# Differential attention: the two maps mixed at raised priority, and the output products issued as three of 128 columns into one sum

## The chip, the cores and the metric

The kernel runs on one core of one Trainium2 chip. The metric is the device time of one execution in microseconds, as the median of several runs. Before the change it is 1921.71 us (three runs, 1919.52 to 1921.93). The engines of a core work side by side and wait for each other through semaphores: TensorE (PE in the profile, with its weight loads shown apart as PEld), VectorE (DVE), ScalarE (ACT), GpSimd (POOL) and SyncE (SP), which issues most of the transfers from memory.

## The reference, cut to what matters

Two decoder layers of width 1024 over 512 tokens. Each layer runs a feed-forward network, a token mixer, a cross-attention into 256 memory tokens, and a second feed-forward network, each followed by a layer norm. The mixer of layer 0 is the differential attention, and the change lies in it alone:

```python
q = rope(q, c5, s5); k = rope(k, c5, s5)          # 8 heads, two maps c = 0, 1 of 64 dims each
s = jnp.einsum('bqhcd,bkhcd->bhcqk', qblk, k).astype(jnp.float32) * scale
s = jnp.where(mask, s, jnp.finfo(jnp.float32).min)
p = jax.nn.softmax(s, axis=-1)
a = p[:, :, 0] - lam * p[:, :, 1]
o = jnp.einsum('bhqk,bkhe->bqhe', a.astype(v.dtype), v)
...
o = o * lax.rsqrt(jnp.mean(jnp.square(o), axis=-1, keepdims=True) + LN_EPS)
o = o * subln_g.astype(jnp.float32) * (1.0 - lam_init)
return o.reshape(B, S, H * 2 * dk).astype(x.dtype) @ w_o
```

## The kernel before, in words

All matrix products keep close to float32 precision by splitting each operand into a high part (rounded to the 4-byte format float32r) and a low part (the rest). A product of two split operands is three matmuls that add into one sum in PSUM: high x high, high x low, low x high (`mm3`, lines 210 to 212). ScalarE makes the high part and VectorE the low part (`split`, lines 125 and 126; `cols_rope`, lines 280 and 283, for the weights of queries and keys).

The differential attention runs two generators side by side (`weave`). The main one (`da_main`) makes values, queries and keys, head by head, and at the end the first half of the output projection. The side one (`da_side`) goes through 8 heads x 4 blocks of 128 queries and issues, each a few steps behind the one before:

- `da_scores`: two maps of scores into PSUM tiles `sc` (lines 1125 and 1126); VectorE adds the mask and finds the row maximum (line 1131), ScalarE takes the exponential with the row sums (line 1134).
- `da_mix`: VectorE computes a reciprocal `rc`, a factor `cf`, and the mixture of both maps, `p[1] * cf + p[0]` (lines 1143 to 1145).
- `da_turn`: TensorE transposes the mixed block `p` into `pt` (line 494); it is split into `a[0]` (high, ScalarE) and `a[1]` (low, VectorE).
- `da_out`: TensorE multiplies it by the values into `po`, for two query blocks per PSUM bank. ScalarE copies half of `po` to `o`, VectorE adds the other half, and ScalarE squares `o` with a row sum into `sq`; after the fourth block GpSimd computes the scale `f`.
- `da_scale`, `da_turn_out`: ScalarE scales `o`, TensorE transposes it, and it is split into `oT`, the operand of the output projection.

The values `v` lie in SBUF as [high | low], 2 x 128 columns side by side. So one matmul with 256 columns yields `a[0]` x high and `a[0]` x low in two separate halves of `po` (line 1166), and a second one with 128 columns adds `a[1]` x high to the first half (line 1167); the two halves are added by VectorE (line 1173). There are 80 such pairs: 8 heads x (1 + 2 + 3 + 4) blocks of keys.

The order of instructions on each engine is set when the kernel is built: a list scheduler takes, among the instructions that it holds to be ready, the one of highest priority, which is by default the order of the program. Code under `self.tc.high_priority()` goes ahead of that. Each engine then works through its own list strictly in that order. TensorE's list in this stage follows the two generators.

PSUM tiles `sc`, `pt` and `po` come from one set of three names with two banks each, taken in turn (`aux`); a bank is used again when everything that reads or writes its tile is done. The squares are written to the first half of `po` (line 1176), a place that is never read.

Of the kernel before, what the change touches and what calls it, by code (L numbers as in the profile page):

```python
# [12 lines left out]
AF = mybir.ActivationFunctionType  # L13
ALU = mybir.AluOpType
# [3 lines left out]
P = 128  # L18
# [91 lines left out]
class Trunk:  # L110
# [80 lines left out]
    def mm(self, name):  # L191
        return self.mmp.tile([P, S], F32, tag="mm", name=name)
# [946 lines left out]
    def da_mix(self, st, i):  # L1139

        nc = self.nc
        p, sm, rc, cf = st.pop(("m", i))
        nc.vector.reciprocal(rc, sm[:, 1:2])
        nc.vector.scalar_tensor_tensor(cf, sm[:, 0:1], self.nlam, rc, ALU.mult, ALU.mult)
        nc.vector.scalar_tensor_tensor(p[0], p[1], cf, p[0], ALU.mult, ALU.add)
        st["p", i] = p[0]

    def da_turn(self, st, i):
# [8 lines left out]
    def da_out(self, st, i):  # L1157
        nc = self.nc
        if i == 0:
            st["o"], st["sq"] = self.tmp("o", (P, NT, P)), self.small("sq", (P, NT))  # L1160
        if i % 2 == 0:
            st["po"] = self.aux("po").rearrange("p (i s e) -> p i s e", i=2, s=2)
        a, o, po, mm = st.pop(("a", i)), st["o"], st["po"], nc.tensor.matmul
        for j in range(i + 1):
            v = st["v"][j][:, st["h"] % 2]
            mm(po[:, i % 2], a[0][:, j], v, start=j == 0, stop=False)
            mm(po[:, i % 2, 0], a[1][:, j], v[:, 0], start=False, stop=j == i)
        if i % 2 == 0:
            return
        o2 = o[:, i - 1 : i + 1]  # L1170
        with self.tc.high_priority():
            nc.scalar.copy(o2, po[:, :, 1])
            nc.vector.tensor_tensor(o2, o2, po[:, :, 0], ALU.add)
        sq = st["sq"]
        for i in range(i - 1, i + 1):
            nc.scalar.activation(
                po[:, 0, 0], o[:, i], AF.Square, scale=float(P**-0.5), accum_out=sq[:, i : i + 1]
            )
        if i < NT - 1:
            return  # L1180

        f, G, s0 = self.small("f", (P, NT)), nc.gpsimd, st["sm"][:, :, 0]
        G.tensor_scalar(f, s0, EPS, None, ALU.mult)
        G.tensor_tensor(f, f, s0, ALU.mult)
        G.tensor_tensor(f, f, sq, ALU.add)
        G.tensor_tensor(f, f, self.mhalf, ALU.pow)
        st["f"] = f
# [446 lines left out]

    def mixer(self, layer, ln):
        if layer == 0:
            bufs = dict(low=4, rt=2, a=4, p=6, o=2, qk=8, _x=0, v=4, oT=11, mask=1)
            with self.other_pools(), self.phase_pool(("v", "v"), "rt", **bufs):
                self.diff_attention(layer, ln)
            self.close_side()  # L1640
        else:
            self.later = ExitStack()
            self.later.enter_context(self.stage_pools(4, dict(raw=2), ("wh", "wl", "mem", "p", "raw")))
            self.to_w(self.later)
            self.kvp = self.later.enter_context(self.pool("kv"))
            bufs = dict(p=4, pw=1, gb=2, _x=0, pooled=16, sq=1)
            with self.phase_pool(("gb", "gb"), "sq", **bufs):
                side = self.pool_mixer(layer, ln)
                with self.tc.high_priority():
                    self.load_memory()  # L1650
                w = self.a["xa_wkv"][layer]
                raws = [self.raw_cols(w, c) for c in (0, D)]
                self.pool_bias()
                next(side)
                self.kv, self.keys, self.kv_bufs = [], [], 10
                self.weave(self.early_kv(layer, ln, 2, raws), side, 850, 8500)
            self.close_side()
# [46 lines left out]
```

## Time and profile before

| | us |
|---|---|
| median of 3 runs | 1921.71 |
| the profiled execution, its own time | 1921.52 |
| its span, first to last instruction | 1919.7 |
| differential attention with scores and outputs running, about 372 to 560 | 188 |

The profile shows the busy time of each engine, groups of equal instructions with their mean duration, who waited for whom, and instructions in order of time. Three points on reading it. A matmul's drawn end is modelled and overlaps the next ones: products of 256 columns start 0.12 us apart while each is drawn 0.28 us long, so what a matmul costs is read from starts, not from durations. A wait is shown as idle time before the instruction that waited, with the one that released it. And in the trace a matmul can be read twice, as its weight load (PEld) and as the product itself.

### The profile page before, as it was taken

To read this page: it belongs to the slowest core of one execution; us is meant where nothing else is said; L and a number is where in the kernel's file an instruction comes from. 1 tells how busy PE (TensorE), PEld (TensorE's weight loads), DVE (VectorE), ACT (ScalarE), POOL (GpSimd) and SP (SyncE) were. 2 spreads that over 40 slices of the span, in tenths; PEclk is the share of its full clock that TensorE was granted. 3 is DMA by queue.
4 is the path that set the end of the run, shared out by engine and by line. 5 is a ranking of instruction groups with operands and counts; after the bars stand their busy time and mean duration, and the time that the engine had idled before them with its cause. 6 is when DMAs were issued, how large, how long until landed. Compare 5 with 4: busy or idle time off the path is not lost.

```text
span 1919.7 us, 32489 instructions
## 1 busy us (share of the span) xinstructions
PE 1895.9 (99%) x13072; PEld 1738.2 (91%) x13072; DVE 1563.6 (81%) x2264; ACT 1023.4 (53%) x1580; POOL 319.8 (17%) x278
## 2 busy tenths in 40 slices
PE   9999999999999999999999999999999999999998
PEld 8999998888878888999998999999899889999997
DVE  7888889888867558889888988898787568998886
ACT  6555454567755435645554655455455436555552
POOL 3112121111210002221220311212130012111210
PEclk9999999999999999999999999999999999999999
DMA  9978772322224327987785587878344437877861
GB/s 250 213 173 179 175 140 78 91 66 88 66 88 154 110 66 195 180 179 162 144 192 180 108 180 164 183 164 183 108 132 132 133 87 162 174 168 167 186 133 55
DMA packets 246743, 277.96 MB, mean 145 GB/s; under 512 B 8256, under 2 KB 212544, under 8 KB 246592
## 3 DMA queue, kind: packets, MB, share of 16 engines
q0 software_dynamic: 92928, 92.29, 31.4%
q1 hardware_dynamic: 153664, 183.59, 29.8%
q8 instruction: 103, 1.69, 0.4%
q14 instruction: 48, 0.39, 0.1%
HBM read 273.75 MB, written 2.10 MB: 144 GB/s over the span
## 4 chain that ended last, share of the span: by engine, by line
PE 78%; DVE 13%; ACT 4%; DMA 2%; issue 2%; POOL 1%; SPq 0%; DVEq 0%; ACTq 0%; POOLq 0%
PE x L210 7%; PE x L211 7%; PE x L212 7%; PE z L212 4%; PE z L210 4%; PE z L211 4%; PE ps L210 4%; PE ps L212 4%; PE ps L211 4%; PE px L210 2%; PE px L212 2%; PE px L211 2%; PE y L212 2%; PE xq L210 1%; PE xq L211 1%
## 5 line engine op out<-in xcount | busy, mean ns | idle before, releaser
L685 POOL DMA_DIRECT2D ra<-in_ffn_w_in_dram x132 | 170.7, 1313 | 982.8 <-DVE wl L692 808.9
L690 ACT CAST wh<-ra 128x1024 fp32r<-128x1024 f32 x176 | 185.1, 1054 | 207.5 <-PE x L211 66.5
L692 DVE TENSOR_TENSOR wl<-ra,wh 128x1024 fp32r<-128x1024 f32 x176 | 213.9, 1220 | 67.1 <-ACT wh L690 66.4
L210 PE MATMUL x<-xe,wh 128*128 128x256 f32 x704 | 195.0, 277 | 0.0
L211 PE MATMUL x<-xe,wh 128*128 128x256 f32 x704 | 194.8, 277 | 0.0
L690 ACT CAST wh<-rc 128x1024 fp32r<-128x1024 f32 x132 | 138.9, 1053 | 104.9 <-PE x L211 40.4
L212 PE MATMUL x<-xe,wl 128*128 128x256 f32 x704 | 194.8, 277 | 0.0
L125 ACT CAST wh<-b 128x1024 fp32r<-128x1024 f32 x112 | 117.8, 1052 | 128.9 <-PE x L211 65.1
L692 DVE TENSOR_TENSOR wl<-rc,wh 128x1024 fp32r<-128x1024 f32 x132 | 159.8, 1218 | 26.8 <-ACT wh L690 26.8
L126 DVE TENSOR_TENSOR wl<-b,wh 128x1024 fp32r<-128x1024 f32 x112 | 136.6, 1220 | 40.2 <-ACT wh L125 40.2
L210 PE MATMUL x<-xh,wh 128*128 128x256 f32 x536 | 148.7, 277 | 0.0
L211 PE MATMUL x<-xl,wh 128*128 128x256 f32 x536 | 148.4, 277 | 0.0
L212 PE MATMUL x<-xh,wl 128*128 128x256 f32 x536 | 148.4, 277 | 0.0
L211 PEld LDWEIGHTS x<-xe,wh 128*128 128x128 f32 x704 | 132.5, 188 | 1.4
L210 PEld LDWEIGHTS x<-xe,wh 128*128 128x128 f32 x704 | 132.2, 188 | 1.3
L212 PEld LDWEIGHTS x<-xe,wl 128*128 128x128 f32 x704 | 132.2, 188 | 0.0
L126 DVE TENSOR_TENSOR wl<-raw,wh 128x1024 fp32r<-128x1024 f32 x64 | 83.0, 1300 | 42.4 <-ACT wh L125 41.6
L211 PEld LDWEIGHTS x<-xl,wh 128*128 128x128 f32 x536 | 100.9, 188 | 0.7
L210 PEld LDWEIGHTS x<-xh,wh 128*128 128x128 f32 x536 | 100.6, 188 | 0.7
L212 PEld LDWEIGHTS x<-xh,wl 128*128 128x128 f32 x536 | 100.6, 188 | 0.0
L125 ACT CAST wh<-raw 128x1024 fp32r<-128x1024 f32 x64 | 66.5, 1049 | 59.3 <-PE xq L211 21.0
L210 PE MATMUL z<-xe,wh 128*128 128x256 f32 x352 | 97.5, 277 | 0.0
(450 smaller groups left out, 6329.1 us busy)
## 6 DMA issues: line engine op xcount, KB each, us to landing
ra<-in_ffn_w_in_dram POOLq DMA_DIRECT2D x132, 512.0 KB, 7.0
rc<-in_ffn_w_in_dram SPq DMA_DIRECT2D x88, 512.0 KB, 5.7
b<-in_ffn_w_out_dram SPq DMA_DIRECT2D x76, 512.0 KB, 4.7
ra<-in_ffn_w_in_dram SPq DMA_DIRECT2D x44, 512.0 KB, 4.7
rc<-in_ffn_w_in_dram POOLq DMA_DIRECT2D x44, 512.0 KB, 8.0
raw<-in_xa_wkv_dram SPq DMA_DIRECT2D x16, 1024.0 KB, 5.4
raw<-in_da_w_qkv_dram SPq DMA_DIRECT2D x16, 512.0 KB, 5.3
raw<-in_xa_wq_dram SPq DMA_DIRECT2D x8, 1024.0 KB, 5.1
```

The costliest lines, as they stand in the source:

```text
L125: self.nc.scalar.copy(hi, src),
L126: self.nc.vector.tensor_sub(lo, src, hi.bitcast(F32)),
L210: mm(out, w[0], x[0], start=start, stop=False, skip_group_check=again)
L211: mm(out, w[0], x[1], start=False, stop=False, skip_group_check=again)
L212: self.last_mm = mm(out, w[1], x[0], start=False, stop=stop, skip_group_check=again)
L685: nc.gpsimd.dma_start(t, source(*block), accum_op=ALU.add)
L690: hi = nc.scalar.copy(v[0], raw)
L692: lo = nc.vector.tensor_sub(v[1], raw, v[0].bitcast(F32))
```

## The change

Three edits, all in the differential attention of layer 0.

1. `da_mix` issues its three VectorE instructions with raised priority.
2. `da_out` accumulates one 128-column result in PSUM with three matmuls of 128 columns per key block (`a[0]` x high, `a[0]` x low, `a[1]` x high) where there were one of 256 and one of 128 columns. `po` takes 2 x 128 columns of the bank instead of 2 x 2 x 128. VectorE's addition (line 1173) is gone; ScalarE's copy reads the finished sum.
3. The squares go to an SBUF tile `squares` of 128 x 128 with one buffer, not to `po`.

```diff
@@ da_mix
-        nc.vector.reciprocal(rc, sm[:, 1:2])
-        nc.vector.scalar_tensor_tensor(cf, sm[:, 0:1], self.nlam, rc, ALU.mult, ALU.mult)
-        nc.vector.scalar_tensor_tensor(p[0], p[1], cf, p[0], ALU.mult, ALU.add)
+        with self.tc.high_priority():
+            nc.vector.reciprocal(rc, sm[:, 1:2])
+            nc.vector.scalar_tensor_tensor(cf, sm[:, 0:1], self.nlam, rc, ALU.mult, ALU.mult)
+            nc.vector.scalar_tensor_tensor(p[0], p[1], cf, p[0], ALU.mult, ALU.add)
@@ da_out
-            st["po"] = self.aux("po").rearrange("p (i s e) -> p i s e", i=2, s=2)
+            st["po"] = self.aux("po")[:, : 2 * P].rearrange("p (i e) -> p i e", i=2)
...
-            mm(po[:, i % 2], a[0][:, j], v, start=j == 0, stop=False)
-            mm(po[:, i % 2, 0], a[1][:, j], v[:, 0], start=False, stop=j == i)
+            mm(po[:, i % 2], a[0][:, j], v[:, 0], start=j == 0, stop=False)
+            mm(po[:, i % 2], a[0][:, j], v[:, 1], start=False, stop=False)
+            mm(po[:, i % 2], a[1][:, j], v[:, 0], start=False, stop=j == i)
...
-            nc.scalar.copy(o2, po[:, :, 1])
-            nc.vector.tensor_tensor(o2, o2, po[:, :, 0], ALU.add)
-        sq = st["sq"]
+            nc.scalar.copy(o2, po)
+        sq, squares = st["sq"], self.tmp("squares", (P, P))
...
-                po[:, 0, 0], o[:, i], AF.Square, scale=float(P**-0.5), accum_out=sq[:, i : i + 1]
+                squares, o[:, i], AF.Square, scale=float(P**-0.5), accum_out=sq[:, i : i + 1]
@@ mixer
-            bufs = dict(low=4, rt=2, a=4, p=6, o=2, qk=8, _x=0, v=4, oT=11, mask=1)
+            bufs = dict(low=4, rt=2, a=4, p=6, o=2, qk=8, _x=0, v=4, oT=11, mask=1, squares=1)
```

The rest of this section shows where instructions stand now. In the changed kernel the lines of `da_mix` are 1144 to 1146 (one more than before), the three products are 1167 to 1169, and the copy and the squares are 1174 and 1177.

TensorE, head 0, the products of the third query block (three key blocks), among the query projection of a later head. Before:

```order
L212 MATMUL q<-xh,wl 128x512
L1166 MATMUL po<-v,a 128x256
L1167 MATMUL po<-v,a 128x128
L1166 MATMUL po<-v,a 128x256
L1167 MATMUL po<-v,a 128x128
L1166 MATMUL po<-v,a 128x256
L1167 MATMUL po<-v,a 128x128
L210 MATMUL q<-xh,wh 128x512
```

With the change:

```order
L212 MATMUL q<-xh,wl 128x512
L1167 MATMUL po<-v,a 128x128
L1168 MATMUL po<-v,a 128x128
L1169 MATMUL po<-v,a 128x128
L1167 MATMUL po<-v,a 128x128
L1168 MATMUL po<-v,a 128x128
L1169 MATMUL po<-v,a 128x128
L1167 MATMUL po<-v,a 128x128
L1168 MATMUL po<-v,a 128x128
L1169 MATMUL po<-v,a 128x128
L210 MATMUL q<-xh,wh 128x512
```

Six matmuls became nine, at the same place. Apart from this, TensorE's list is the same in both kernels up to the last head.

VectorE, an earlier head's last query block (its scores are the 128x512 ones): `rc`, `cf` and `p` are the mix, `a<-pt,a` the low part of a transposed block that TensorE waits for. Before:

```order
L1143 RECIPROCAL rc<-sd 128x1
L1144 SCALAR_TENSOR_TENSOR cf<-sd,nlam,rc 128x1
L1145 SCALAR_TENSOR_TENSOR p<-p,cf 128x512
L126 TENSOR_TENSOR a<-pt,a 128x256
L1131 ISA p,mx<-sc,mask 128x128
```

With the change:

```order
L1144 RECIPROCAL rc<-sd 128x1
L1145 SCALAR_TENSOR_TENSOR cf<-sd,nlam,rc 128x1
L126 TENSOR_TENSOR a<-pt,a 128x256
L1146 SCALAR_TENSOR_TENSOR p<-p,cf 128x512
L1131 ISA p,mx<-sc,mask 128x128
```

The low part of `a`, which has raised priority in both kernels, now stands ahead of the mixture.

VectorE, third query block of a later head (the block is 384 columns wide). `rt<-q` and `wl<-raw` belong to the main generator: the rotation of the next head's query, and low parts of weights. Before:

```order
L1143 RECIPROCAL rc<-sd 128x1
L1083 STREAM_SHUFFLE rt<-q 128x512
L1084 TENSOR_TENSOR rt<-q,ropeC 128x512
L126 TENSOR_TENSOR a<-pt,a 128x128
L1086 TENSOR_TENSOR rt<-rt 128x512
L1173 TENSOR_TENSOR o<-o,po 128x256
L1144 SCALAR_TENSOR_TENSOR cf<-sd,nlam,rc 128x1
L126 TENSOR_TENSOR wl<-raw,wh 128x1024
...
L1097 SCALAR_TENSOR_TENSOR qk<-rt,qk 64x512 x2
L1145 SCALAR_TENSOR_TENSOR p<-p,cf 128x384
```

With the change:

```order
L1144 RECIPROCAL rc<-sd 128x1
L1145 SCALAR_TENSOR_TENSOR cf<-sd,nlam,rc 128x1
L1146 SCALAR_TENSOR_TENSOR p<-p,cf 128x384
L1083 STREAM_SHUFFLE rt<-q 128x512
L126 TENSOR_TENSOR a<-pt,a 128x128
L1084 TENSOR_TENSOR rt<-q,ropeC 128x512
L126 TENSOR_TENSOR wl<-raw,wh 128x1024
L1086 TENSOR_TENSOR rt<-rt 128x512
```

The three instructions of the mix now stand together, ahead of the rotation and the weights; the addition has left the list.

At the end of the stage, in the last head, the four transposes of `o` stand two products earlier in TensorE's list: the first comes right after an L212 where before an L210 and an L211 followed that L212. SyncE's list is the same, and on GpSimd the scale `f` of two heads changes places with a neighbour.

## The prediction

> **What bounds the kernel now.** I read the busy times first, then the windows of the differential attention, then TensorE's waits there, and last single starts.
>
> ```profile
> PE 1895.9 (99%) x13072; PEld 1738.2 (91%) x13072; DVE 1563.6 (81%) x2264; ACT 1023.4 (53%) x1580; POOL 319.8 (17%) x278
> 440.00:480.00 40.00, 40.00 (x211) 33.75 (x210) 37.97 (x92) 29.11 (x72) 7.68 (x8) 1.00 0.26 79
> 372.00:560.00 188.00, 181.16 (x1089) 157.62 (x1088) 160.31 (x410) 129.58 (x353) 32.61 (x45) 1.00 0.26 79
> ```
>
> TensorE (first line; columns of the windows: length, then PE, PEld, DVE, ACT, POOL busy, granted clock 1.00) leaves 23.8 us of the whole span idle, and 6.84 us of the 188 us in which the changed code runs. VectorE is busy for 160 of those 188 and for 38 of 40 at its fullest, but TensorE hardly stops for it. So TensorE bounds this stage: what it is given to do is added to the time, and only its few stalls can be won back. These are all of them above 0.1 us, 9 in number (columns: total us, times, longest):
>
> ```profile
> PE pt L494 <- DVE p L1145: 2.6, 2, 1.4
> PE sc L1125 <- ACT po L1176: 1.5, 2, 0.8
> PE pt L494 <- ACT o L1192: 1.1, 1, 1.1
> PE sc L1125 <- ACT qk L1112: 0.9, 2, 0.7
> PE po L1167 <- DVE a L126: 0.6, 1, 0.6
> PE po L1166 <- ACT a L125: 0.2, 1, 0.2
> ```
>
> Their sum is 6.9 us. A drawn matmul hides a little more of each stall: it is 0.28 us long while the next one normally starts 0.12 us later, so each stall costs 0.16 us beyond its row, 9 x 0.16 = 1.4, together 8.3 us. That is the most that any rearrangement of VectorE and ScalarE can give back here.
>
> **The third product.** What 128-column products cost back to back shows in the first scores, what the pair costs now in two pairs of `po` a little later:
>
> ```profile
> 385.47 0.28 PE L212 MATMUL v<-wh,xl 128*128 128x256 f32 x1
> 385.59 0.22 PE L1125 MATMUL sc<-qk 128*128 128x128 f32 x1
> 385.64 0.28 PE L1126 MATMUL sc<-low,qk 128*128 128x128 f32 x1
> 385.76 0.27 PE L1125 MATMUL sc<-qk 128*128 128x128 f32 x1
> 385.87 0.28 PE L1126 MATMUL sc<-low,qk 128*128 128x128 f32 x1
> 385.98 0.33 PE L210 MATMUL v<-wh,xh 128*128 128x256 f32 x1
> 386.15 0.28 PE L211 MATMUL v<-wl,xh 128*128 128x256 f32 x1
> ...
> 388.48 0.28 PE L1166 MATMUL po<-v,a 128*128 128x256 f32 x1
> 388.60 0.22 PE L1167 MATMUL po<-v,a 128*128 128x128 f32 x1
> 388.66 0.33 PE L1166 MATMUL po<-v,a 128*128 128x256 f32 x1
> 388.83 0.22 PE L1167 MATMUL po<-v,a 128*128 128x128 f32 x1
> 388.89 0.33 PE L210 MATMUL v<-wh,xh 128*128 128x256 f32 x1
> 389.06 0.28 PE L211 MATMUL v<-wl,xh 128*128 128x256 f32 x1
> ```
>
> After a 128-column product the next one can start 0.05 to 0.06 us later, but then the one after that starts late, because its weights were not there. So a group is measured from its first start to the second start behind it, less one 256-column product (0.12). Four products of 128 columns: 386.15 - 385.59 - 0.12 = 0.44, or 0.11 each. Two pairs: 389.06 - 388.48 - 0.12 = 0.46, or 0.23 a pair. A 128-column product thus costs nearly what one of 256 columns does. Each matmul brings its own weight load (both counts in the first row are 13072), also where two neighbours share the weights, as L210 and L211 do, so the second product gets nothing for free. A triple costs 3 x 0.11 = 0.33, 0.10 more than the pair; for 80 pairs **+8.2 us** on the bounding engine (0.103 x 80). Bounds: at 0.12 each, the spacing of 256 columns, it is 0.13 x 80 = 10.4; at 0.058, the spacing that a 128-column product shows alone, a triple is 0.17 against 0.12 + 0.06 for the pair, and the change costs nothing.
>
> [...]
>
> **What lies beside.** These durations are from the groups by shape of that stage:
>
> ```profile
> L1173 DVE TENSOR_TENSOR o<-o,po 128x256 f32<-128x256 f32 x16 | 6.7, 416 | 0.9 <-ACT o L1172 0.9
> L1176 ACT ACTIVATE po<-o 128x128 f32<-128x128 f32 x32 | 8.9, 278 | 12.3 <-DVE o L1173 11.9
> L1192 ACT ACTIVATE o<-o,f 128x128 f32<-128x128 f32 x32 | 11.1, 394 | 7.8 <-POOL f L1186 7.8
> L1143 DVE RECIPROCAL rc<-sd 128x1 f32<-128x1 f32 x32 | 5.1, 159 | 11.5 <-ACT p L1134 11.4
> ```
>
> The 16 additions take 6.7 us off VectorE, and ScalarE's 11.9 us of waiting for them ends; both engines have room (160 and 130 of 188), so by themselves they move nothing. The copy reads 256 columns of PSUM as before. Squares in SBUF are not in this trace: they cost 278 ns into PSUM, and the nearest instruction from SBUF to SBUF of that shape is the scaling at 394, so 0 to 0.116 x 32 = 3.7 us more on ScalarE, covered by its 58 us of free time; without that cover only the last two squares of the last head lie open, 0.2 us. [...] No transfer is issued or moved.
>
> **What the nine stalls become.** Each is taken with its hidden 0.16 us.
>
> ```profile
> 375.63 0.55 DVE L1131 CUSTOM_DVE_ANT_0 p<-sc,mask 128x384 f32<-128x384 f32 x1
> 437.43 0.16 DVE L1143 RECIPROCAL rc<-sd 128x1 f32<-128x1 f32 x1 [2.63 <-ACT p L1134]
> 437.88 0.75 DVE L1145 SCALAR_TENSOR_TENSOR p<-p,cf 128x512 f32<-128x512 f32 x1
> 438.55 0.42 DVE L126 TENSOR_TENSOR a<-pt,a 128x256 fp32r<-128x256 f32 x1
> ...
> 482.61 0.21 DVE L1144 SCALAR_TENSOR_TENSOR cf<-sd,nlam,rc 128x1 f32<-128x1 f32 x1
> 482.75 1.22 DVE L126 TENSOR_TENSOR wl<-raw,wh 128x1024 fp32r<-128x1024 f32 x1
> 485.21 1.40 DVE L1097 SCALAR_TENSOR_TENSOR qk<-rt,qk 64x512 fp32r<-64x512 f32 x2
> 486.65 0.62 DVE L1145 SCALAR_TENSOR_TENSOR p<-p,cf 128x384 f32<-128x384 f32 x1
> ...
> 557.27 0.39 PE L210 MATMUL ps<-qk,oT 128*128 128x512 f32 x1
> 557.50 0.39 PE L211 MATMUL ps<-qk,oT 128*128 128x512 f32 x1
> 558.98 0.33 PE L494 MATMUL pt<-ident,o 128*128 128x128 f32 x1 [1.10 <-ACT o L1192]
> ```
>
> - *The mixture is late (2.6 in two).* The longer stall, 1.4 + 0.16, is the very first block: one mask instruction (0.55) now stands behind the mixture but another reciprocal ahead of it, so I take 0.3 won. The other, 1.2 + 0.16, ends at 486.65; its mixture waited behind weights (1.22), two masks and a query (1.40), and the new list puts it ahead of all of these: 1.4 won.
> - *The bank of `po` is late (1.5 in two).* TensorE waited for the squares to leave the bank that new scores need. Now the copy alone frees it, and no addition stands between: both go, 1.5 + 0.3 = 1.8 won.
> - *The low part of `a` (0.6).* It stood behind a mixture of 0.75; the two change places: 0.7 won. The 0.2 at the high part before it stays.
> - *The last head's `o` (1.1).* The copy's successor comes without the addition (about 0.5 us with its handovers), but the transposes stand two products of 0.23 earlier in TensorE's list, which asks that much sooner: nothing won.
> - *The new keys (0.9 in two).* The chain of their rotation is not touched: nothing won.
>
> That is 0.3 + 1.4 + 1.8 + 0.7 = **4.2 us won**. Against it stands the raised priority itself. A reciprocal waits for an exponential, and all that is queued behind it on VectorE waits too: rotations of queries and keys, low parts of weights and of `a`, which TensorE waits for next. VectorE already stands 11.4 us at that instruction, 13 times, and once for 2.6. Bounds: below, a gain, since TensorE gets slower and VectorE has 6.7 us less to do, so that the last stalls shrink too (up to 8.3 - 4.2 = 4.1 more won); above, one such wait of 2.6 that reaches TensorE whole. Nearest is the key chain's present stall of 0.9, one more of which I put at **+1.0 us**.
>
> Sum: the profiled execution's own 1921.5 (span 1919.7 and 1.8 around it; the median of the runs, 1921.7, is the same within 0.2) + 8.2 - 4.2 + 1.0 = **1926.5 us**. Later stages start 5 us later and are otherwise the same.
>
> **The rivals.** (a) *All stalls go, and the change comes out not slower.* With the additions gone and TensorE itself 8 us slower, VectorE and ScalarE run ahead from the first head on, at every one of the nine places: 1921.5 + 8.2 - 8.3 = 1921.4. It decides from 4.4 us of stalls won upward, where the time comes under the +0.2% line. For it: no stall is longer than 1.4. Against: the first block and the last head have no lead to build on, and the key chain starts from TensorE's own product, so it does not get earlier when TensorE gets slower. (b) *Columns count, weight loads hide.* The product between other products costs its 0.058 alone, and the triple is free: 1921.5 - 4.2 + 1.0 = 1918.3. For it speaks that weight loads are drawn overlapping and PEld is busy for only 158 of 188 here; against it the scores' row. (c) *The reciprocal blocks VectorE.* Raised, it stands at the head of the list before its exponential is done, and two or three waits of the 2.6 kind reach TensorE as late queries, keys or weights: 1921.5 + 8.2 - 4.2 + 2.5 x 2.6 = 1932. For it: VectorE is at 38 of 40 in places; against: 6.7 us less work there, and of 11.4 us of such waits now almost nothing reaches TensorE. That the change doesn't do what it says falls away: the lists show the extra products and the missing additions.
>
> **How the numbers follow.** The forecast gets 0.63, (a) 0.15, (b) 0.05, (c) 0.14, and 0.03 is left for what I do not see. The range 1921.5 to 1931.5 runs from nearly all stalls gone to a triple at its upper price (10.4) with almost nothing won net; it leaves out (b) and the upper half of (c). A measurement of this kernel can tell about 0.2%, 3.8 us, from no change, so the lines are 1917.9 and 1925.5. Within them fall (a), half of (b) and a fifth of the forecast, where a stall or two more goes: 0.28 in all. Below 1917.9 lies the other half of (b): 0.03. The rest, 0.69, is slower.
>
> **What would show it.** TensorE has 80 matmuls more, three starts of `po` in a row take 0.33 us against 0.23 for the pair, and TensorE's busy time in the stage grows by about 8 us. No stall of scores behind the squares remains, and the stall at 485 is gone; those of the first block, the new keys and the last head stay. VectorE's busy time falls by 6.7 us in the stage, and its time at the reciprocal grows. Wrong would be a triple at 0.25 or less (then (b)), idle time of TensorE in the stage under 1 us (then (a)) or over 8 us with rows for late queries, keys or weights (then (c)).

## The result, and the profile after

The changed kernel takes **1926.53 us** (median of 10 runs, 1925.07 to 1928.08) against 1921.24 for the kernel before (10 runs beside it, 1919.29 to 1922.49): a ratio of 1.0031 with a 95% interval of 1.0023 to 1.0039. It is slower by 5.3 us. The forecast was 1926.5, slower. The profiled execution has an own time of 1926.19.

The page's head and busy times of the changed kernel:

```profile
span 1924.4 us, 32618 instructions
PE 1903.1 (99%) x13152; PEld 1745.7 (91%) x13152; DVE 1558.7 (81%) x2248; ACT 1024.8 (53%) x1580; POOL 320.2 (17%) x278
```

A window of its differential attention (columns as before: length, then PE, PEld, DVE, ACT, POOL busy, granted clock, DMA share, GB/s):

```profile
480.00:520.00 40.00, 37.85 (x240) 33.66 (x239) 34.33 (x86) 28.53 (x80) 10.26 (x12) 0.96 0.16 53
```

80 matmuls more, 16 VectorE instructions fewer. TensorE's busy time grew by 7.2 us (1895.9 to 1903.1), its idle time fell from 23.8 to 21.3, and the two give the span's 4.7. The granted clock of 480 to 520 is 0.96, where it was 1.00: something happened there that the forecast did not have.

What the triple costs shows where a pair was read before, in TensorE's timeline of the changed kernel (start, drawn duration, line):

```profile
386.88 0.22 PE L1167 MATMUL po<-v,a 128*128 128x128 f32 x1
386.94 0.28 PE L1168 MATMUL po<-v,a 128*128 128x128 f32 x1
387.06 0.28 PE L1169 MATMUL po<-v,a 128*128 128x128 f32 x1
...
387.67 0.28 PE L211 MATMUL v<-wl,xh 128*128 128x256 f32 x1
```

Left out are a second triple and one product of 256 columns. By the same measure as in the prediction, two triples take 387.67 - 386.88 - 0.12 = 0.67, so 0.334 each; the pair took 0.23. The change is 0.104 x 80 = 8.3 us.

TensorE's waits in the differential attention of the changed kernel (total us, times, longest):

```profile
PE po L1167 <- ACT a L125: 1.9, 1, 1.9
PE pt L494 <- ACT o L1193: 1.1, 1, 1.1
PE pt L494 <- DVE p L1146: 0.9, 1, 0.9
PE po L1169 <- DVE a L126: 0.3, 1, 0.3
PE sc L1125 <- ACT qk L1112: 0.2, 1, 0.2
```

Nine waits became five. Gone are the scores behind the squares, the mixture at 485 and nearly all of the new keys; left are the first block (0.9 instead of 1.4) and the last head (1.1). New is the longest of them, for the high part of `a`. Its place is visible on three engines. ScalarE first:

```profile
480.40 0.31 ACT L1177 ACTIVATE squares<-o 128x128 f32<-128x128 f32 x1
480.61 0.19 ACT L1177 ACTIVATION_READ_ACCUMULATOR squares<-o 128x1 f32 x1
484.39 0.40 ACT L1193 ACTIVATE o<-o,f 128x128 f32<-128x128 f32 x1 [3.59 <-POOL f L1187]
484.70 1.27 ACT L1096 ACTIVATE qk<-rt 64x512 fp32r<-64x512 f32 x2
485.99 0.72 ACT L1134 ACTIVATE p<-p,mx 128x512 f32<-128x512 f32 x1
...
488.00 0.35 ACT L125 CAST a<-pt 128x256 fp32r<-128x256 f32 x1
```

The first scaling of a finished head (L1193) stands right behind the squares in ScalarE's list and waits 3.59 us for the factor `f`. Behind it stand a query, the exponentials, and the high part of `a`. GpSimd, which makes `f`, at that time:

```profile
480.48 1.30 POOL L1085 TENSOR_TENSOR rt<-rt,ropeS 128x512 f32<-128x512 f32 x1 [8.88 <-DVE rt L1083]
481.73 1.19 POOL L1186 TENSOR_TENSOR f<-f,sq 128x4 f32<-128x4 f32 x1
483.00 1.36 POOL L1187 TENSOR_TENSOR f<-f,mhalf 128x4 f32<-128x4 f32 x1
```

It is finishing a rotation when the squares are ready, and then takes 2.6 us for two instructions of four columns. In the kernel before, ScalarE stood only 0.77 us at that point, because the squares themselves came 2.02 us late behind VectorE's addition, as its timeline there shows:

```profile
482.73 0.28 ACT L1176 ACTIVATE po<-o 128x128 f32<-128x128 f32 x1 [2.02 <-DVE o L1173]
...
483.04 0.61 ACT L1096 ACTIVATE qk<-rt 64x512 fp32r<-64x512 f32 x1
...
485.37 0.41 ACT L1192 ACTIVATE o<-o,f 128x128 f32<-128x128 f32 x1 [0.77 <-POOL f L1186]
```

There both queries stood ahead of the scaling (the second starts at 483.97); now the scaling stands ahead of both. ScalarE asks for `f` 3.8 us earlier (at 480.8 against 484.6), and GpSimd delivers it only 1.0 us earlier (484.39 against 485.37). What it does to TensorE in the changed kernel:

```profile
486.15 0.40 PE L212 MATMUL q<-xh,wl 128*128 128x512 f32 x1
488.40 0.33 PE L1167 MATMUL po<-v,a 128*128 128x128 f32 x1 [1.85 <-ACT a L125]
...
490.58 0.63 PE L211 MATMUL q<-xl,wh 128*128 128x512 f32 x1
491.01 0.63 PE L212 MATMUL q<-xh,wl 128*128 128x512 f32 x1
```

The last two lines show the second part of the loss: two products of 512 columns start 0.43 us apart, where they otherwise start 0.233 apart (median of 300 in this stage). The windows of the changed kernel around it say why (the figure behind the five engines is the clock):

```profile
488.00:490.00 2.00, 1.30 (x6) 1.16 (x7) 1.50 (x6) 1.33 (x6) 0.00 (x0) 0.79 0.00 0
490.00:492.00 2.00, 2.00 (x7) 1.61 (x7) 1.70 (x6) 1.78 (x5) 0.22 (x1) 0.50 0.00 0
```

After the stall the granted clock fell to a half for about 3.4 us. That lengthens the work in it by some 1.7 us.

**Where the 5.3 us come from.** Pairing each TensorE instruction of one profiled execution with the same one of the other, and following the difference of their starts from step to step: triples +8.3; stalls gone -6.15 (first block 0.42, keys 1.19, both parts of `a` 1.37, scores behind squares 1.79, mixture 1.38); new +4.2 (the stall for the high part of `a` 2.0, for the low part 0.5, both with what the drawn ends hide, and the half clock 1.7); about -0.4 in small steps. The sum is 5.9 for the stage. The spans differ by less, 4.7, since TensorE reached the stage 1.3 us earlier in the second execution, before any changed instruction; the medians' 5.3 lies between.

### The profile page after: what moved, and what is told of

It reads as the page before. It is cut to its first block, busy times and chain, and to the rows that moved or that the text cites. A ratio compares the mean times of both kernels' runs of the same rounds, so it can differ in the third digit from the quotient of the medians.

```text
span 1924.4 us, 32618 instructions
## 1 busy us (share of the span) xinstructions
PE 1903.1 (99%) x13152; PEld 1745.7 (91%) x13152; DVE 1558.7 (81%) x2248; ACT 1024.8 (53%) x1580; POOL 320.2 (17%) x278
## 4 chain that ended last, share of the span: by engine, by line
PE 81%; DVE 12%; ACT 3%; DMA 2%; issue 1%; POOL 1%; SPq 0%; DVEq 0%; ACTq 0%; POOLq 0%
PE x L211 7%; PE x L210 7%; PE x L212 6%; PE z L212 4%; PE z L210 4%; PE z L211 4%; PE ps L210 3%; PE ps L212 3%; PE ps L211 3%; PE px L210 2%; PE px L212 2%; PE px L211 2%; PE y L212 2%; PE xq L210 1%; PE xq L211 1%; PE xq L212 1%
## 5 line engine op out<-in xcount | busy, mean ns | idle before, releaser
L210 PE MATMUL x<-xe,wh 128*128 128x256 f32 x704 | 194.8, 277 | 0.0
L211 PE MATMUL x<-xe,wh 128*128 128x256 f32 x704 | 194.6, 276 | 0.0
L212 PE MATMUL x<-xe,wl 128*128 128x256 f32 x704 | 194.5, 276 | 0.0
L210 PE MATMUL x<-xh,wh 128*128 128x256 f32 x536 | 148.6, 277 | 0.0
L211 PE MATMUL x<-xl,wh 128*128 128x256 f32 x536 | 148.3, 277 | 0.0
L212 PE MATMUL x<-xh,wl 128*128 128x256 f32 x536 | 148.3, 277 | 0.0
L211 PEld LDWEIGHTS x<-xe,wh 128*128 128x128 f32 x704 | 132.3, 188 | 1.4
L210 PEld LDWEIGHTS x<-xe,wh 128*128 128x128 f32 x704 | 132.1, 188 | 1.3
L212 PEld LDWEIGHTS x<-xe,wl 128*128 128x128 f32 x704 | 132.2, 188 | 0.0
L211 PEld LDWEIGHTS x<-xl,wh 128*128 128x128 f32 x536 | 100.8, 188 | 0.7
L210 PEld LDWEIGHTS x<-xh,wh 128*128 128x128 f32 x536 | 100.6, 188 | 0.7
L212 PEld LDWEIGHTS x<-xh,wl 128*128 128x128 f32 x536 | 100.7, 188 | 0.0
L210 PE MATMUL z<-xe,wh 128*128 128x256 f32 x352 | 97.4, 277 | 0.0
```

The source lines that it names most:

```text
L210: mm(out, w[0], x[0], start=start, stop=False, skip_group_check=again)
L211: mm(out, w[0], x[1], start=False, stop=False, skip_group_check=again)
L212: self.last_mm = mm(out, w[1], x[0], start=False, stop=stop, skip_group_check=again)
```

## The experiments

"After" is the changed kernel, edits 1 to 3 are numbered as in the section on the change, and each ratio is to the kernel before, run beside it.

### 1. The third product alone

```diff
-            mm(po[:, i % 2], a[0][:, j], v, start=j == 0, stop=False)
+            mm(po[:, i % 2, 0], a[0][:, j], v[:, 0], start=j == 0, stop=False)
+            mm(po[:, i % 2, 1], a[0][:, j], v[:, 1], start=False, stop=False)
```

> The kernel before with one edit: the 256-column product of da_out is issued as two of 128 columns into the same two halves of po; addition, squares and priorities stay. Theory (a matmul of up to 256 columns costs its weight load, 0.11 us): a triple of starts takes 0.33 us, 0.10 more than the pair, 80 times, so +8.3 us on TensorE and about 1929 to 1930 us, a little less where stalls shrink because TensorE is slower (down to 1927). Rival (columns count, weight loads hide): a triple costs what the pair does, 1921 us.

Measured: 1930.86 us against 1921.92, ratio 1.0046 (1.0033 to 1.0058). The first start of two triples in its timeline, and the second start behind them:

```profile
387.20 0.22 PE L1166 MATMUL po<-v,a 128*128 128x128 f32 x1
...
387.99 0.28 PE L211 MATMUL v<-wl,xh 128*128 128x256 f32 x1
```

387.99 - 387.20 - 0.12 = 0.67 again, with the addition, the squares and the priorities as they were. The price of the triple belongs to the matmuls. The whole step is 8.9 us, but the stalls did not all stay. TensorE's waits in the stage fell from 6.9 us in nine to 5.5 in seven: the later mixture's is gone and `a` has 0.4 instead of 0.8, while one grew (scores behind squares, one of 1.7). With what the drawn ends hide this is 1.7 us won because TensorE got slower, a small part of rival (a)'s 8.3. In the profiled execution the clock fell to a half here too, at 488.7, and took about as much back.

### 2. The raised priority alone

```diff
+        with self.tc.high_priority():
+            nc.vector.reciprocal(rc, sm[:, 1:2])
...
```

> The kernel before with the raised priority of da_mix alone. Theory (the priority takes away the late mixtures and the late low part of a): three stalls of TensorE go or shrink, -0.4 at the first block, -1.4 at the later mixture, -0.9 at the low part, so about 1918.5 us; the waits for the bank of po behind the squares (1.8 with what the drawn ends hide), for new keys (1.2) and for the last head's o (1.3) stay. Rival (the reciprocal blocks VectorE): VectorE's time at the reciprocal grows beyond 11.4 us and TensorE waits for late queries, keys or weights: 1922 us or more.

Measured: 1920.73 us, ratio 0.9995 (0.9986 to 1.0004), a miss. TensorE's waits of this kernel:

```profile
PE po L1167 <- ACT a L125: 1.0, 2, 0.9
PE pt L494 <- DVE p L1146: 0.9, 1, 0.9
PE po L1168 <- DVE a L126: 0.6, 1, 0.6
...
PE pt L494 <- DVE a L126: 0.5, 1, 0.5
```

The later mixture's wait is gone, the first block's is 0.9, and the squares' are gone too. But the 0.6 for the low part of `a` stays, and TensorE waits anew at the next steps of the same chain, for `a` (0.9 and 0.5). VectorE's list here still has the mixture ahead of the low part:

```profile
435.39 0.75 DVE L1146 SCALAR_TENSOR_TENSOR p<-p,cf 128x512 f32<-128x512 f32 x1
436.06 0.42 DVE L126 TENSOR_TENSOR a<-pt,a 128x256 fp32r<-128x256 f32 x1
```

So the exchange of these two instructions that the section on the change shows is not the priority's work. Experiment 5, without the priority, has it; it comes with edit 2. What a wait at the mixture cost is not won when the splitting behind it is late as well.

### 3. The squares into SBUF alone

```diff
-                po[:, 0, 0], o[:, i], AF.Square, ...
+                squares, o[:, i], AF.Square, ...
```

> The kernel before with the squares in SBUF alone; the pair of products and the addition stay. Theory (the bank of po was held by the squares): the two waits of scores for the squares go, -1.8 us, about 1919.4 us, and a square takes 0.31 us where it took 0.28. Rival (the bank is held by the addition as well, and the wait only gets another name): rows of scores waiting for the addition, 1921 us.

Measured: 1922.71 us, ratio 1.0002 (0.9994 to 1.0011), a miss again. Its longest waits on TensorE:

```profile
PE pt L494 <- DVE p L1145: 3.6, 2, 2.3
```

No scores wait for squares any more, as expected; the next wait, for the mixture, grew from 1.2 to 2.3 us. TensorE runs ahead to where the next thing is late.

### 4. After, with the scaling queued later on ScalarE

If ScalarE's order makes the new stall, the scaling of a head put behind the last exponential of the next head must remove it.

```diff
-                nc.scalar.activation(
+                st["exp", i] = nc.scalar.activation(
                     p[m], p[m], AF.Exp, ...
...
-        for i in range(NT):
-            self.nc.scalar.activation(o[:, i], o[:, i], AF.Copy, ...)
+        nxt = self.heads[min(st["h"] + 1, DA_H - 1)][1]
+        with self.tc.issue_after(nxt["exp", NT - 1].ins):
+            for i in range(NT):
+                self.nc.scalar.activation(o[:, i], o[:, i], AF.Copy, ...)
```

> The changed kernel with one more edit: ScalarE's scaling of a head's o is queued behind the exponential of the next head's last block. Theory (in the changed kernel ScalarE stands at the scaling for GpSimd's f, 3.6 us at 480.8, and with it the query, the exponentials and the high part of a that TensorE waits 1.85 us for; TensorE's clock then falls to half for some 4 us, 1.8 us more): this wait and the half clock both go, the granted clock is 1.00 from 480 to 520, and the time is 1926.5 - 3.8 = 1922.7 us. Rival (the high part of a was late for another reason, such as the exponentials waiting for VectorE's maxima): the wait of about 1.9 us stays, 1926.5 us.

Measured: 1923.67 us, ratio 1.0010 (1.0001 to 1.0019), 2.9 us below after by the medians and 3.5 when each is set against the kernel before that ran beside it. ScalarE and then TensorE at the place of the stall, in this kernel:

```profile
482.43 1.28 ACT L1096 ACTIVATE qk<-rt 64x512 fp32r<-64x512 f32 x2 [2.74 <-DVE rt L1086]
...
485.17 0.68 ACT L1195 ACTIVATE o<-o,f 128x128 f32<-128x128 f32 x2
485.75 0.35 ACT L125 CAST a<-pt 128x256 fp32r<-128x256 f32 x1
```

```profile
485.72 0.40 PE L212 MATMUL q<-xh,wl 128*128 128x512 f32 x1
486.16 0.33 PE L1167 MATMUL po<-v,a 128*128 128x128 f32 x1
```

GpSimd is as slow there as in after (1.18 and 1.36 us for the same two instructions), but nobody stands for it: query and exponentials go first, `a` is there in time, and TensorE takes 0.44 us from L212 to L1167, not 2.25. The half clock is gone as well:

```profile
480.00:520.00 40.00, 39.66 (x267) 35.61 (x266) 35.14 (x90) 29.72 (x81) 10.38 (x12) 1.00 0.16 53
```

So the new loss was ScalarE waiting for `f`, and the half clock that followed. Three waits above 0.1 us are left in the stage, 2.3 us, and the kernel is still 1.75 us over the one before: the triple costs more than the stalls give back.

### 5. After without the raised priority

```diff
-        with self.tc.high_priority():
-            nc.vector.reciprocal(rc, sm[:, 1:2])
+        nc.vector.reciprocal(rc, sm[:, 1:2])
...
```

> The changed kernel without the raised priority (edits 2 and 3 alone). Theory (the priority takes away the late mixtures): the stall at the first block grows by 0.4, the mixture of the 384-column block at 485 is late again (1.4), and a low part of a stands behind a mixture again (0.9): 1926.5 + 2.7 = 1929 us. Rival (with 16 additions gone VectorE has room, and the mixtures come in time in the order of the program): 1926.5 us or less.

Measured: 1927.28 us, ratio 1.0029 (1.0017 to 1.0040): the same as after. Waits, on TensorE:

```profile
PE po L1166 <- ACT a L125: 1.7, 1, 1.7
PE pt L494 <- DVE p L1145: 1.4, 1, 1.4
...
PE pt L494 <- DVE cf L1144: 0.9, 1, 0.9
```

The stall for the high part of `a` is here without the priority, so the priority did not make it. The mixture's stall at 485 is gone without it, too: the priority was not needed for that in after. What the priority improves is the first block's 1.4 and the 0.9 in the last line, at 515 us. That the half clock, which this kernel's profiled execution does not have, takes this back in after is argued, not shown.

### 6. After with the squares in PSUM

```diff
-                squares, o[:, i], AF.Square, ...
+                po[:, 0], o[:, i], AF.Square, ...
```

> The changed kernel with the squares written to po again (edits 1 and 2 alone). Theory (once the addition is gone the squares follow the copy at once, at 480 to 481, 2.5 us before the scores that need the bank): no change, 1926.5 us. Rival (the bank is late again): a wait of scores for the squares comes back, up to 1.8 us, 1928.3 us.

Measured: 1927.17 us, ratio 1.0029 (1.0017 to 1.0040), no change from after, with a stall of 1.8 for the high part of `a` and the half clock as there. With the addition gone, the place of the squares no longer matters.

### 7. The pair and the addition kept, edits 1 and 3 made

```diff
+        with self.tc.high_priority():
...
-                po[:, 0, 0], o[:, i], AF.Square, ...
+                squares, o[:, i], AF.Square, ...
```

> The kernel before with edits 1 and 3, without edit 2: the pair of 256 and 128 columns and the addition stay. Theory (each of the two edits alone freed TensorE from one wait only to run into the next, a mixture that comes late; together both are gone, and no third product is paid): first block -0.4, scores behind squares -1.7, mixture -1.4, and some of the waits for keys and for the low part of a, together about -4 us, 1918 us. Rival (the additions on VectorE keep the chain late): as with the priority alone, 1920.7 us.

Measured: 1921.62 us, ratio 0.9998 (0.9989 to 1.0007), a miss: without the triple's 8.3 us the other two edits are worth nothing. At the place of after's 3.6 us ScalarE waits 0.9 us for `f`, and TensorE then 1.0 for the high part of `a`.

### 8. The same with the scaling queued later

The edit of experiment 4 on the kernel of experiment 7.

> As the run before this one, and ScalarE's scaling of o queued behind the next head's last exponential. Theory (ScalarE's stand at the scaling delays the high part of a, 1.0 us of TensorE's time with the priority alone): 1 us less than without it, 1917 us. Rival (with the addition in place the scaling is not ahead of anything urgent): the same as without it.

Measured: **1917.60 us** (1914.89 to 1918.77), ratio 0.9971 (0.9962 to 0.9980), faster than both kernels. Its waits on TensorE, and its windows:

```profile
PE pt L494 <- ACT o L1195: 1.1, 1, 1.1
PE pt L494 <- DVE p L1146: 0.9, 1, 0.9
PE ps L210 <- DVE X L362: 0.3, 1, 0.3
PE po L1168 <- DVE a L126: 0.3, 1, 0.3
PE pt L494 <- DVE a L126: 0.2, 1, 0.2
```

```profile
372.00:565.00 193.00, 190.11 (x1132) 165.69 (x1131) 163.87 (x419) 131.05 (x355) 34.66 (x46) 1.00 0.25 77
```

TensorE is idle for 2.9 us of these 193. The first block and the last head make 2.0 of the 2.8 us of waits listed.

### 9. The kernel before with the scaling queued later

The edit of experiment 4 on the kernel before, nothing else.

> The kernel before with the queued scaling alone (no raised priority, squares in po, pair and addition). Theory (the three edits free TensorE only together: the bank of po and the late mixtures are waits of their own): the waits for squares (1.7) and mixtures (2.6) stay, the time is 1920 to 1922 us, clearly above the 1917.6 of the run with all three. Rival (the order on ScalarE is the root of all of them): about 1918 us.

Measured: 1918.74 us, ratio 0.9984 (0.9975 to 0.9993), faster by some 3.6 us. Its waits on TensorE:

```profile
PE pt L494 <- DVE p L1145: 2.6, 2, 1.4
PE pt L494 <- ACT o L1194: 1.1, 1, 1.1
PE sc L1125 <- ACT po L1176: 0.6, 2, 0.3
PE ps L210 <- DVE X L362: 0.3, 1, 0.3
```

The waits for the keys and for `a` are gone and the squares' fell from 1.5 to 0.6; the mixture's stay. ScalarE's order already cost in the kernel before most of what could be won. Edits 1 and 3, worth nothing without it (experiment 7), may win a little once it is mended: 1918.74 here, 1917.60 with them. That is not shown: these two were not run beside each other, and the intervals of their ratios overlap.

### 10. After without its second product

```diff
-            mm(po[:, i % 2], a[0][:, j], v[:, 1], start=False, stop=False)
```

> The changed kernel without its second product, high part of a x low part of v (that term of the sum is left out, the result is less precise); two products of 128 columns remain. Theory (each matmul costs its weight load, 0.11 us): 80 x 0.11 = 8.9 us less than the changed kernel, 1917.6 us, and no dearer than the kernel before with its pair of 256 and 128 columns in the same number of matmuls. Rival (columns count, 0.058 us for 128): 80 x 0.058 = 4.6 us less, 1921.9 us.

Measured: 1919.81 us, ratio 0.9988 (0.9980 to 0.9997). Groups of two, four, six and eight products take 0.222, 0.442, 0.668 and 0.889 us (from the first start to the second start behind the group, less one product of 256 columns, 0.121 in these groups): 0.111 a product in groups of each of these lengths, so 8.9 us for 80, and in none of them 0.058. The time fell by 6.7 us against after by the medians and by 7.8 when each is set against the kernel before beside it; a wait for keys of 1.5 us appeared on TensorE, and the clock's half stretch is here as well.

## Why the prediction was right

The number came out within 0.1 us, but not all of its terms did. The large one held. Of the two smaller ones, the gain was 1.95 us too small and the loss 3.2 too small; that these nearly cancelled is luck, and so is the 0.1. Even "slower" hung on the loss that was not foreseen: with ScalarE's stall and the half clock removed (experiment 4), the kernel is 1.75 us slower, which the prediction's own line of 0.2% counts as no change.

- **TensorE bounds, and weight loads are paid by the product.** Right: +8.2 predicted, +8.3 by starts, and experiments 1 and 10 give 0.334 a triple and 0.111 a product each by itself. After's page has as many weight loads as products (13152 each), and in its triples the loads start 0.11 us apart (387.00, 387.11, 387.22, 387.33), as the products do; that the load sets the price is the author's reading of this spacing. Rival (b) falls: a gap of 0.058 stands only behind the first product of a group (386.88 to 386.94), and no group shows it as a price.
- **What lies beside.** Right. Squares in SBUF cost 310 ns instead of 278, within the bound of 394, and nothing came of it (experiment 6). VectorE's additions are gone; its busy time over the whole program fell by 4.9 us, less than their 6.7. "By themselves they move nothing" was wrong, though; see the last term below.
- **Stalls won, 4.2 predicted, 6.15 measured.** The mixture (1.4; 1.38 measured), the squares (1.8; 1.79) and the first block (0.3; 0.42) were sized well, and the last head's 1.1 stayed. (One time is misread: 486.65 is where the mixture of the later stall starts; the stall ends at 487.32.) "The new keys: nothing won" failed: 1.19 went. So did "the 0.2 at the high part stays": `a` gave 1.37 in all against 0.7. The keys had been put down to a chain that the change does not touch, the high part had no reason given. Experiment 9 shows what they hung on: with only ScalarE's scaling put later they go as well. The 0.7 for the low part came, but not by the reason given: in experiments 4 and 9 the mixture stands ahead of it at this place and the wait is gone all the same, and in 2 and 7, which have the priority, the 0.6 stays.
- **The list puts the mixture ahead at 485.** The stall went, but it is gone in experiment 5 too, without the priority, and in experiment 2, where the priority works alone, the gain passed to a wait for `a`. Right outcome, and a reason that was not the needed one.
- **The raised priority, +1.0.** This is the step that failed. VectorE's time at the reciprocal did grow, as predicted, from 11.4 to 18.4 us, but not through the priority: it is 18.0 in experiment 5 without it and 12.8 in experiment 2 with it alone. Of TensorE's waits only the 0.3 for the low part of `a` stands behind such a reciprocal, and it is 0.3 in experiment 5 too. Without the priority the time is the same. The loss came from another engine: +4.2, by ScalarE, whose scaling stands first in its list and waits for GpSimd's `f`. The prediction had noted ScalarE's 7.8 us at the scaling and the end of its 11.9 us of waiting for additions, and concluded "by themselves they move nothing". With the addition gone, a scaling was listed ahead of the queries, and ScalarE asked for `f` 3.8 us earlier than before, while GpSimd gave it 1.0 us earlier; a free engine became a blocked one. Every kernel without the addition in which the scaling was not moved has a stall of 1.4 to 1.9 us for the high part of `a` (after, 5, 6, 10); with the addition kept the longest is 1.0 (1, 2, 3, 7). At that place ScalarE waits 3.6 us for `f` in after, 5 and 6 and 2.0 in 10, but 0.1 to 0.9 in 1, 2, 3 and 7. Experiment 4 shows that the scaling's place makes the stall. That the scheduler listed the scaling earlier *because* the addition was gone is argued from these, not traced in its decisions.
- **Rivals.** (c) had the right shape, a raised or early instruction at the head of an in-order list, on the wrong engine. (a) had its mechanism for 6.15 of 8.3 us; it fell by the stall that replaced them. Experiment 4 is nearest to (a), 1.75 us above its kernel before. (Among the chances, the three parts named for "no change" add up to 0.30, not 0.28.)

What stays open: how much of the loss is the half clock. The 1.7 us are read from the starts of one execution; experiment 4 removes stall and half clock together, and the kernel of experiment 5 has a stall of 1.7 us without the half clock and is no faster than after, as it keeps two stalls that after has not or has shorter, 1.4 us by their rows. The runs' mean granted clocks give a hint. All runs of experiments 2, 4, 7 and 8 show 0.999, and one such stretch takes 0.0009 off (half of 3.413 us in 1924); of after's ten runs four show 0.999 and six 0.998 or 0.997, with medians of 1925.8 and 1927.0 us. So the half clock seems not to come in every execution, and to cost about a microsecond where it comes, but runs of one kind scatter by more than that.

## What to carry to other kernels

Splitting a matmul into narrower ones on the engine that bounds was paid per product here (0.111 us for 128 columns, where one of 256 takes 0.118): a VectorE addition that lies in free time is no price for it. When an instruction is removed ahead of an in-order engine's list, read what now stands first there and what it waits for (here a scaling, 3.59 us), also on an engine with a third of its time free. A small wait taken away came back at the next step of the same chain in experiments 2, 3 and 7 (0.9, 2.3 and 1.0 us); one instruction that blocks a list, put behind the urgent ones, was worth some 3 us in the kernel before (experiment 9), where the three edits together cost 5.3.

## What the hardware showed that was not expected

**After a stall of 1.85 us the clock stood at a half for 3.413 us.** In the traces of after and of experiments 1, 6 and 10 the clock's own records show 0.5 for 3.413 us, once each, and 1.00 at all other times of this stage. The drop begins 484.69 us after the first moment of full clock in after, 1 and 6, and 481.28 in 10, which is 142 and 141 times 3.4133. At the end of the kernel, behind TensorE's last product, a drop begins 1908.05 us after that moment in the kernel before and 1914.88 in after, 559 and 561 times the same length. Counted in windows of that length from that moment, the window ahead of the drop in this stage held 2.15 us of TensorE idle time in after, 2.12 in experiment 6, 1.65 in experiment 1 and 1.63 in experiment 10; windows with up to 1.37 us did not lead to a drop, nor one with 1.66 (experiment 5). This is the stall of experiment 3 that left the clock alone:

```profile
486.38 0.55 PE L494 MATMUL pt<-ident,p 128*128 128x128 f32 x3 [2.27 <-DVE p L1145]
```

2.27 us are longer than after's 1.85, but it lay across the border of two such windows with 1.31 and 0.96 in them. That about half a window idle is where it turns, and that the place of a stall decides as much as its length, is an estimate from these few cases. Seven of the eleven runs of experiment 3 show a mean clock of 0.998, so in other executions the same stall may have fallen within one window; no trace shows it.

**GpSimd's small addition was six times as long at one place.** The addition of 128 x 4 numbers (`f`) took 1.19 us in after and 0.20 in the kernel before, at 484.02; it comes eight times in each, and the other fourteen took 0.20 as well. Beside the slow one ran a VectorE instruction that was slow as well:

```profile
481.02 1.84 DVE L126 TENSOR_TENSOR wl<-raw,wh 128x1024 fp32r<-128x1024 f32 x1
```

The two ended within 0.1 us of each other, at 482.92 and 482.86. The same subtraction took 1.22 in the kernel before at 482.75, with no GpSimd instruction beside it. Whether the two hold each other up is not shown: no run here separates them.
